# Cutting the last two result banks of a weight-gradient matmul differently: 384 + 128 columns, and two stores of 256

## The chip, the cores and the metric

One core of a Trainium2 chip. The metric is device microseconds of one execution.

The runs scatter by some 0.8 us, and the change was expected to be worth a few hundredths. So most of the argument uses an interval inside one trace, the **closing stretch**: from the start of VectorE's addition for the next to last bank to the end of the span. All that the change touches lies in it. A store **lands** when the trace shows its last completion signal.

## The reference

```python
batch, m, k, n = 16, 512, 1024, 768          # input [16, 512, 1024], grad_output [16, 512, 768], float32
grad_weight = np.einsum('bmk,bmn->kn', input, grad_output)   # [1024, 768], float32
```

That is a sum over 8192 rows, or 64 slices of 128 rows, for a result of 1024 x 768.

## The kernel before

Inputs are rounded to bf16 while they are loaded. TensorE runs 512 of the 768 columns ("wide") as eight banks of 128 x 512, one for each block of 128 result rows, and the other 256 columns ("narrow") transposed. Partial sums are added from the accumulation banks to `acc` in on-chip memory as the slices arrive. The last 14 slices (50 to 63) of the wide part are done bank by bank, so that finished banks can be stored while the others run. This loop is the whole end of the program:

```python
    def add_out(dst, src):
        nc.vector.tensor_add(out=dst, in0=src, in1=dst)
    # ... (cut: loads, rounding, the main accumulation, the narrow part and its 4 stores from ScalarE)
    for k in range(KS):                                   # KS = 8, NA = 512, NB = 256
        slices = range(parts["A" if k < KS // 2 else "B"].done, S)
        pieces = [(0, NA)] if k < KS - 1 else [(0, 256), (256, 384), (384, NA)]
        for c0, c1 in pieces:
            name = free.pop(0)
            bank = psum.tile([P, NA], f32, name=name)[:, 0 : c1 - c0]
            for s in slices:
                wide_mm(bank, k, s, s == slices[0], s == slices[-1], c0, c1)
            add_out(acc[:, k, c0:c1], bank)
            free.append(name)
            W = NB if k < 6 else c1 - c0
            for c in range(c0, c1, W):
                nc.sync.dma_start(out=OUT[:, k, c : c + W], in_=acc[:, k, c : c + W])
```

So banks 0 to 5 are stored in two halves, bank 6 in one store of 512, bank 7 in three pieces: 12 + 1 + 3 = 16 stores on SyncE's queue.

Of the kernel before, what the change touches and what calls it, by code (L numbers as in the profile page):

```python
# [9 lines left out]
NA = 512  # L10
# [16 lines left out]
def kernel(  # L27
# [13 lines left out]
    KS = K // P  # L41
    NB = N - NA
# [74 lines left out]
    def add_out(dst, src):  # L117
        nc.vector.tensor_add(out=dst, in0=src, in1=dst)  # L118
# [7 lines left out]
    def wide_mm(bank, k, s, start, stop, c0=0, c1=NA):  # L126
        nc.tensor.matmul(  # L127
            bank, xs[s][:, k * P : (k + 1) * P], gwide[s][:, c0:c1], start=start, stop=stop
        )
# [105 lines left out]

    for k in range(KS):
        slices = range(parts["A" if k < KS // 2 else "B"].done, S)
        pieces = [(0, NA)] if k < KS - 1 else [(0, 256), (256, 384), (384, NA)]
        for c0, c1 in pieces:
            name = free.pop(0)  # L240
            bank = psum.tile([P, NA], f32, name=name)[:, 0 : c1 - c0]
            for s in slices:
                wide_mm(bank, k, s, s == slices[0], s == slices[-1], c0, c1)
            add_out(acc[:, k, c0:c1], bank)
            free.append(name)
            W = NB if k < 6 else c1 - c0
            for c in range(c0, c1, W):
                nc.sync.dma_start(out=OUT[:, k, c : c + W], in_=acc[:, k, c : c + W])

# [29 lines left out]
```

## Time and profile before

| | kernel before |
|---|---|
| median of the first three runs | 176.0 us (175.91 to 176.1) |
| span in the profile | 174.27 us |
| TensorE busy | 97% of the span |
| next to last bank's addition starts | 168.41 |
| last bank's three additions start | 169.94, 170.72, 171.50 |
| last store issued, landed | 171.82, 173.36 |

The table is read as a relay. TensorE ends an accumulation, VectorE adds it within 0.02 us, SyncE issues the store 0.03 us after the addition ends, and the store lands 1.5 us or more later. Only the last runner of each kind is on the path to the end. The lines themselves are in the prediction.

### The profile page before, as it was taken

Reading aid. Unit: us, or ns where it says so; the run is one execution under the profiler, and the core shown is the slowest. Engines: PE = TensorE matmul, PEld = TensorE weight load, DVE = VectorE, ACT = ScalarE, POOL = GpSimd, SP = SyncE. Lnnn points to the kernel's source line nnn. Section 1 sums busy time; section 2 is a strip of 40 time slices with the busy share of each in tenths; the row PEclk is TensorE's granted clock in tenths of the full one; section 3 lists DMA queues with packets and bytes.
Section 4 is the critical chain, followed back from the end, with each engine's and each line's share of the span. In section 5 each row is a group of like instructions: output and inputs, shape, how many; then the busy total and the mean of one; then the engine's idle time right before and its main releaser. Section 6 shows DMA issues by size and latency. Waiting matters only on the chain.

```text
span 174.3 us, 2013 instructions
## 1 busy us (share of the span) xinstructions
PE 169.9 (97%) x793; PEld 78.4 (45%) x808; DVE 61.3 (35%) x103; ACT 6.2 (4%) x12; POOL 66.7 (38%) x129
## 2 busy tenths in 40 slices
PE   8999999999999999999999999999999999999993
PEld 3444444444444444444444444444444444444463
DVE  0655582883940039300000662200560003931122
ACT  2640000000000000000000000000000000000000
POOL 7444434444444444444444444444274200000000
PEclk9999999999999999999999999999999999999999
DMA  5999999999999999999999999999999990085623
GB/s 192 276 208 209 207 209 208 208 208 209 207 208 209 207 208 210 207 209 209 206 209 208 208 210 207 207 209 208 207 209 209 207 202 11 0 190 160 170 86 120
DMA packets 25048, 33.35 MB, mean 191 GB/s; under 512 B 6480, under 2 KB 16592, under 8 KB 25040
## 3 DMA queue, kind: packets, MB, share of 16 engines
q0 software_dynamic: 18000, 28.65, 89.9%
q10 hardware_dynamic: 4448, 2.10, 4.7%
q1 hardware_dynamic: 2592, 2.49, 4.2%
q8 instruction: 6, 0.10, 0.2%
q14 instruction: 2, 0.02, 0.0%
HBM read 58.72 MB, written 3.15 MB: 355 GB/s over the span
## 4 chain that ended last, share of the span: by engine, by line
PE 97%; issue 0%; DVE 0%
PE bank L127 63%; PE bank L134 32%; PE bank L81 3%; DVE acc L118 0%
## 5 line engine op out<-in xcount | busy, mean ns | idle before, releaser
L127 PE MATMUL bank<-gt,xt 128*128 128x512 bf16 (+2 forms) x515 | 108.3, 367 | 0.5
L127 PEld LDWEIGHTS <-xt 128*128 128x128 bf16 x524 | 50.2, 98 | 57.2
L118 DVE TENSOR_TENSOR acc<-bank,acc 128x512 f32<-128x512 f32 (+2 forms) x62 | 37.9, 667 | 73.4 <-PE bank L127 72.9
L134 PE MATMUL bank<-xt,gt 128*128 128x512 bf16 x242 | 54.8, 379 | 0.3
L97 POOL DMA_DIRECT2D xt<-in_input_dram x62 | 33.1, 533 | 38.7 <-DMA xt<-in_input_dram 36.5
L92 POOL DMA_DIRECT2D gt<-in_grad_output_dram x63 | 33.8, 536 | 31.2 <-DMA gt<-in_grad_output_dram 24.9
L134 PEld LDWEIGHTS <-gt 128*128 128x128 bf16 x252 | 24.6, 98 | 29.7
L118 DVE TENSOR_TENSOR acct<-bank,acct 128x512 f32<-128x512 f32 x24 | 15.7, 682 | 30.0 <-PE bank L134 29.9
L81 PE MATMUL bank<-const-bfloat16-1.0 128*128 128x512 bf16 (+1 forms) x12 | 4.6, 574 | 0.8 <-PEq L263 0.8
L81 PEld LDWEIGHTS <-const-bfloat16-1.0 128*128 128x128 bf16 x12 | 1.6, 140 | 3.5 <-issue 3.5
L122 DVE COPY acc<-bank 128x512 f32<-128x512 f32 x4 | 2.7, 687 | 1.0 <-PE bank L127 1.0
L180 DVE STREAM_TRANSPOSE turned<-acct 128x512 f32<-128x512 f32 x4 | 2.9, 715 | 0.1
L127 PEld LDWEIGHTS <-x 128*128 128x128 bf16 x16 | 1.6, 98 | 1.9 <-DVE x L107 0.2
L107 DVE CAST g<-gf 128x256 bf16<-128x256 f32 x2 | 0.6, 290 | 4.7 <-DMA gf<-in_grad_output_dram 4.7
L124 ACT COPY acc<-bank 128x512 f32<-128x512 f32 x4 | 2.1, 589 | 1.3 <-PE bank L127 1.3
L127 PE MATMUL bank<-gt,x 128*128 128x512 bf16 x8 | 2.1, 379 | 0.0
L127 PE MATMUL bank<-g,x 128*128 128x512 bf16 x8 | 2.0, 398 | 0.0
L122 DVE COPY acct<-bank 128x512 f32<-128x512 f32 x2 | 1.3, 686 | 1.3 <-PE bank L134 1.3
L107 ACT CAST x<-xf 128x256 bf16<-128x256 f32 x4 | 1.4, 409 | 0.0
L107 ACT ACT_TABLE_LOAD x1 | 1.3, 1283 | 1.7 <-PEq L263 1.7
L124 ACT COPY acct<-bank 128x512 f32<-128x512 f32 x2 | 1.1, 588 | 1.5 <-PE bank L134 1.5
L107 DVE CAST x<-xf 128x256 bf16<-128x256 f32 (+1 forms) x5 | 1.0, 260 | 0.0
(8 smaller groups left out, 3.3 us busy)
## 6 DMA issues: line engine op xcount, KB each, us to landing
xt<-in_input_dram POOLq DMA_DIRECT2D x62, 256.0 KB, 8.5
gt<-in_grad_output_dram POOLq DMA_DIRECT2D x63, 192.0 KB, 8.5
out_dram<-acc SPq DMA_DIRECT2D x13, 128.0 KB, 2.7
xf<-in_input_dram ACTq DMA_DIRECT2D x2, 512.0 KB, 5.1
out_dram<-turned ACTq DMA_DIRECT2D x4, 256.0 KB, 3.4
gf<-in_grad_output_dram SPq DMA_DIRECT2D x1, 256.0 KB, 3.9
out_dram<-acc SPq DMA_DIRECT2D x1, 256.0 KB, 2.0
gf<-in_grad_output_dram SPq DMA_DIRECT2D x1, 128.0 KB, 4.7
```

The costliest lines, as they stand in the source:

```text
L81: nc.tensor.matmul(wps[:, 0:cols], ones, nc.const_aps.tensor(1.0, (P, cols), bf16), start=True, stop=True,)
L92: nc.gpsimd.dma_start(out=gt, in_=G[s * P : (s + 1) * P, :])
L97: nc.gpsimd.dma_start(out=xs[s], in_=X[s * P : (s + 1) * P, :])
L107: copy(out=dst[:, c0:c1], in_=src[:, c0:c1])
L118: nc.vector.tensor_add(out=dst, in0=src, in1=dst)
L122: nc.vector.tensor_copy(out=dst, in_=src)
L124: nc.scalar.copy(out=dst, in_=src)
L127: nc.tensor.matmul(bank, xs[s][:, k * P : (k + 1) * P], gwide[s][:, c0:c1], start=start, stop=stop)
L134: nc.tensor.matmul(bank, gnarrow[s].rearrange("p (r t) -> p t r", t=NT)[:, t], xs[s][:, h * NA : (h + 1) * NA], start=start, stop=stop,)
L180: nc.vector.transpose(out=turned[:, h * hb : (h + 1) * hb, :, t], in_=dst.rearrange("p (b r) -> p b r", r=SQ),)
```

## The change

The last bank is cut in two pieces in place of three (fewer instructions and stores, the same last piece of 128), and the next to last bank goes out in two stores of 256, like those before it.

```diff
-        pieces = [(0, NA)] if k < KS - 1 else [(0, 256), (256, 384), (384, NA)]
+        pieces = [(0, NA)] if k < KS - 1 else [(0, 384), (384, NA)]
...
-            W = NB if k < 6 else c1 - c0
+            W = NB if k < KS - 1 else c1 - c0
```

## The prediction

> **What bounds the kernel now.** I read the page first (busy shares, the chain that ended last), then the end of the run: the chain in order of time, VectorE's timeline for the last 6 us, the SyncE queue, and the table of stores. The page settles the main body:
>
> ```profile
> PE 169.9 (97%) x793; PEld 78.4 (45%) x808; DVE 61.3 (35%) x103; ACT 6.2 (4%) x12; POOL 66.7 (38%) x129
> ...
> PE 97%; issue 0%; DVE 0%
> PE bank L127 63%; PE bank L134 32%; PE bank L81 3%; DVE acc L118 0%
> ```
>
> TensorE is busy 97% of the 174.3 us span and is the whole chain but for one VectorE addition. Only two things can therefore move the time: TensorE's stream, and what follows its last matmul. The chain in order of time shows where the stream stops:
>
> ```profile
> 164.76 6.72 PE bank L127 x58
> 171.48 0.02 issue
> 171.50 0.29 DVE acc L118
> ```
>
> The last matmul ends at 171.48, the last addition takes 0.29 us, and the span runs to 174.3. So there is a **tail** of 2.8 us: addition, last store, closing of the program. The change touches only what lies after about 168.4 us. VectorE's additions mark there when each accumulation is complete, because each starts within 0.02 us of its last matmul:
>
> ```profile
> 165.39 0.69 DVE L118 TENSOR_TENSOR acc<-bank,acc 128x512 f32<-128x512 f32 x1 [2.33 <-PE bank L127]
> 168.41 0.69 DVE L118 TENSOR_TENSOR acc<-bank,acc 128x512 f32<-128x512 f32 x1 [2.33 <-PE bank L127]
> 169.94 0.42 DVE L118 TENSOR_TENSOR acc<-bank,acc 128x256 f32<-128x256 f32 x1 [0.84 <-PE bank L127]
> 170.72 0.29 DVE L118 TENSOR_TENSOR acc<-bank,acc 128x128 f32<-128x128 f32 x1 [0.36 <-PE bank L127]
> 171.50 0.29 DVE L118 TENSOR_TENSOR acc<-bank,acc 128x128 f32<-128x128 f32 x1 [0.49 <-PE bank L127]
> ```
>
> Every addition waited for TensorE (the brackets), so VectorE is never behind. Differences of these starts, divided by the 14 slices of an accumulation (the trace counts 14 matmuls of 256 columns and 28 of 128), give the real cost of one matmul, which the modelled durations (379, 272 and 219 ns) do not:
> - 512 columns: (168.41 - 165.39) / 14 = 215.7 ns
> - 256 columns: (169.94 - 168.41) / 14 = 109.3 ns
> - 128 columns: (170.72 - 169.94) / 14 = 55.7 ns, and the same for the third piece.
>
> The line through the first and the last is 0.4167 ns per column plus 2.4 ns per matmul; at 256 it gives 109.1 ns. So the time goes by columns, and a piece more costs almost nothing.
>
> The last store is issued at 171.82, just after the last addition ends:
>
> ```profile
> 171.82 0.33 SPq L248 DMA_DIRECT2D out_dram<-acc  x1
> ```
>
> and the table of stores says how long each size takes from issue to landing:
>
> ```profile
> out_dram<-acc SPq DMA_DIRECT2D x1, 256.0 KB, 2.0
> ...
> out_dram<-acc SPq DMA_DIRECT2D x2, 64.0 KB, 1.5
> ```
>
> So the last 64 KB lands at about 173.3. From there to 174.3 is 1.0 us of closing, and from the span to the measured time another 1.7 us (the profiled run took 176.04). The change touches neither.
>
> **What the Trainium skill says, and whether the trace agrees.**
> - "TensorE: Matmul & The Clock Gate", section "Back-to-back issue gap", gives N / 2.4 + 2.5 ns for a warm matmul of N columns. The trace agrees: 215.7, 109.3 and 55.7 ns against 215.8, 109.2 and 55.8. The same section says that a stream of weight load and matmul pairs sustains about 81 ns at 128 columns; here the stream does 55.7, although each weight load shows 98 ns of busy time, so the loads hide even at the smallest size.
> - "Perfetto Trace Analysis", section "DMA Optimizations", says that splitting a transfer may let parts start sooner where DMA engines are idle. The DMA share in the page's slices is 9 for most of the run, but between stores at the end the engines rest (no byte moves from 168.9 to 169.6 us), so nothing there needs a split to find room.
> - "DMA: Bandwidth & Descriptors", section "Queues, rings and completion order", says that each DMA engine takes descriptors in ring order. The last store can therefore stand behind the one before it. In the trace of before no two of the last stores overlap, so it does not show this.
>
> **The change part by part.** All numbers below are on the clock of the old trace.
>
> *1. Next to last bank: two stores of 256 columns for one of 512.* Adds one issue of 0.33 us on SyncE: 169.13 to 169.46, then 169.46 to 169.79. SyncE next has work at 171.27 (below), so the issue is hidden. The bytes are the same; the old store moved its 256 KB between about 169.9 and 170.75, well before the next data. Worth 0 either way.
>
> *2. Last bank, matmuls.* Removed: 14 of 256 columns, 14 of 128. Added: 14 of 384. The last 14 of 128 stay. A 384 column matmul should take 384 x 0.4167 + 2.4 = 162.4 ns. So 14 x 162.4 = 2.27 us replaces 14 x (109.3 + 55.7) = 2.31 us: 14 matmuls' fixed 2.4 ns, **0.035 us less**, all on the path. That is the whole gain.
>
> *3. Additions.* Removed: 0.42 and 0.29 us. Added: one of 384 columns, estimated by a line through 292 ns at 128, 425 at 256 and 692 at 512 as 0.56 us. It starts at 168.41 + 2.27 = 170.68 and ends at 171.24. The last addition is due at 170.68 + 0.78 = 171.46, so VectorE is free 0.2 us before. Hidden, and the last addition is the same 128 columns and 0.29 us: done at 171.75.
>
> *4. Stores of the last bank.* Before: 128, 64, 64 KB. After: 192 and 64 KB. The 192 KB store is issued at 171.27 and holds SyncE to 171.60; the last is ready at 171.78. No wait at the issue. At the transfer it is closer: in the DMA view of these windows the first byte moves about 0.80 us after the issue, and the last about 1.3 us after it for 128 KB and 1.6 us for 256 KB. By interpolation the 192 KB store moves between 172.07 and about 172.72; the last store's bytes are due from 172.58. DMA engines that are late with the first would delay their share of the second: an estimated **0 to 0.15 us more**, by this overlap.
>
> *5. Tail.* The same last piece, so the same 1.5 us to landing and 1.0 us of closing.
>
> The sum is -0.035 + (0 to 0.15), taken as -0.035 + 0.05 = about +0.02 us on 176.0. That is no change.
>
> **The rivals.**
> - *The 192 KB store holds the last one up.* For it: the overlap just worked out, and that 0.51 us, against 0.78 before, now separates the last two issues. Against it: only the engines that are late with the larger store can pass the delay on. It would make 176.1 us, at the very most 176.2.
> - *Fewer instructions save real time*, 14 matmuls, 14 weight loads and one addition. For it: each weight load is busy for 98 ns; if the 14 removed loads were exposed at that, 1.4 us would go, and the result would be 174.6. Against it: 128 column matmuls already start every 55.7 ns, so the loads cannot be exposed.
> - *VectorE or SyncE becomes the bound at the end* through the wider addition or the later store. For it: VectorE's margin before the last addition shrinks from 0.49 to about 0.2 us, SyncE's to the same. Against it: both are still positive. If both failed by 0.1 us: 176.1.
> - *A store waits for an earlier one's semaphore.* In the compiled order of the changed kernel, the new second store of the next to last bank waits for a store issued about 9 us before; the slowest SyncE store of the old trace took 4.7 us to land, so the wait is over. If it were not, only that store would move, and it has over 2 us to spare.
>
> **Range and chances.** Centre 176.0. The known terms span -0.04 to +0.15; the runs of before span 175.91 to 176.1, and another set of runs can sit a little off. I give 175.7 to 176.3. Two per cent is 3.5 us; the whole region that the change touches, from 168.4 to the end of the stores, is 5 us, so neither side is reachable by an effect that the trace shows: faster 0.01, same 0.98, slower 0.01.
>
> **What would show each step right or wrong in the changed profile.** Step 2: the addition of 384 columns starts 2.27 us after the addition of the bank before it (3.05 us to the last addition; 3.09 before). Step 3: that addition takes 0.56 us and the last one still shows idle time before it that TensorE ended. Steps 1 and 4: SyncE shows four issues from 169.1 on, as before, two of them back to back, and the last within 0.05 us of the last addition's end; landing of the last 64 KB still about 1.5 us; 1.6 or more would mean that it queued behind the 192 KB. The prediction would be wrong if a 384 column matmul did not follow the line, or if a transfer of 1536 bytes a row went much slower than its neighbours of 1024 and 2048.

## More of the kernel before

Every run quoted is of the undisturbed (fast) state, or a single run whose granted TensorE clock was at least 0.998 of full. Single runs serve for their profile, not for their time.

## The result, and the profile after

| | before | after |
|---|---|---|
| median | 175.99 us (175.78 to 176.47, 6 runs) | 176.12 us (175.83 to 176.55, 6 runs) |
| ratio | | 1.0006, 95% interval 0.9987 to 1.0024 |
| span of the profiled run | 174.27 us | 174.78 us |
| closing stretch | 5.864 us | 5.860 us |

The ratio is the mean time of the changed kernel's fast runs over that of the other's fast runs of the same rounds, so not quite the ratio of the medians. The time is the same.

The page of the changed kernel keeps its shape, with 14 matmuls fewer:

```profile
PE 170.4 (97%) x779; PEld 77.8 (45%) x794; DVE 61.2 (35%) x102; ACT 6.2 (4%) x12; POOL 66.4 (38%) x129
```

VectorE's last additions after the change (start, duration, operation; the bracket is the idle time before it and what ended it):

```profile
165.90 0.69 DVE L118 TENSOR_TENSOR acc<-bank,acc 128x512 f32<-128x512 f32 x1 [2.33 <-PE bank L127]
168.92 0.69 DVE L118 TENSOR_TENSOR acc<-bank,acc 128x512 f32<-128x512 f32 x1 [2.33 <-PE bank L127]
171.19 0.56 DVE L118 TENSOR_TENSOR acc<-bank,acc 128x384 f32<-128x384 f32 x1 [1.58 <-PE bank L127]
171.97 0.29 DVE L118 TENSOR_TENSOR acc<-bank,acc 128x128 f32<-128x128 f32 x1 [0.22 <-PE bank L127]
```

The three steps between starts say it all: 3.02 for the bank before (as before), 2.27 for 14 matmuls of 384 columns, 0.78 for 14 of 128. The last addition still waited 0.22 us for TensorE, so VectorE did not become the bound. The last store and the table of stores (operation, size, us from issue to landing):

```profile
172.29 0.33 SPq L248 DMA_DIRECT2D out_dram<-acc  x1
```

```profile
out_dram<-acc SPq DMA_DIRECT2D x1, 192.0 KB, 1.9
...
out_dram<-acc SPq DMA_DIRECT2D x1, 64.0 KB, 1.6
```

The last 64 KB took 1.6 us where it took 1.5 before (1.567 and 1.536 in the trace's landing records). The DMA view of the last 2.9 us of stores shows what differs; each digit is the busy share of the DMA engines in a fortieth of the window, in tenths. Before, from 170.8 us:

```profile
DMA  0000007999851016983000000279730000000000
```

After, from 171.3 us:

```profile
DMA  6200000000000000006999999889830000000000
```

Before, three stores (128, 64, 64 KB) move with rests between them. After, the 192 KB and the 64 KB run into each other (the first two digits are the end of the stores before). In the DMA records the first bytes of the 64 KB move at 173.14 and the last of the 192 KB at 173.30. That is the overlap of the prediction, at its small end: 0.03 us. It repeats: in the runs below, a 64 KB last store behind one of 192 KB lands in 1.556 to 1.591 us (3 runs), and one with a rest before it in 1.521 to 1.536 (6 runs).

**Where the profiled runs differ.** All stamps of the changed trace are 0.51 us later than the old ones, and that is no effect of the change. The chain in order of time has the same first matmuls on real data in both (start, duration, what), first the kernel before:

```profile
5.42 1.95 PE bank L127 x8
```

and then the changed kernel:

```profile
5.42 2.45 PE bank L127 x8
```

These eight matmuls come 160 us ahead of the first changed instruction. The trace's clock record has full speed from 5.63 us on in one run and from 6.73 on in the other; 1.1 us more at half speed (an estimate of the speed before, from the 0.5 that the record shows after the last matmul) would cost 0.55 us. Over the 14 traces the next to last bank's addition starts anywhere from 168.17 to 168.92, with TensorE's instructions ahead of it the same in all. The moment of the clock grant is of the right size for this, but it does not explain all of it: in the run with four banks in 4 stores each (below) full speed is on record from 3.40 us on, and that addition still starts at 168.48. For the timed runs it is not shown at all, as these have no traces.

### The profile page after: what moved, and what is told of

The parts are those of the page before. It is cut to its first block, busy times and chain, and to the rows that moved or that the text cites. A ratio compares the mean times of both kernels' runs of the same rounds, so it can differ in the third digit from the quotient of the medians.

```text
span 174.8 us, 1983 instructions
## 1 busy us (share of the span) xinstructions
PE 170.4 (97%) x779; PEld 77.8 (45%) x794; DVE 61.2 (35%) x102; ACT 6.2 (4%) x12; POOL 66.4 (38%) x129
## 4 chain that ended last, share of the span: by engine, by line
PE 97%; issue 0%; DVE 0%
PE bank L127 63%; PE bank L134 31%; PE bank L81 3%; DVE acc L118 0%
## 5 line engine op out<-in xcount | busy, mean ns | idle before, releaser
L127 PEld LDWEIGHTS <-xt 128*128 128x128 bf16 x510 | 49.4, 98 | 58.0
L127 PE MATMUL bank<-g,x 128*128 128x512 bf16 x8 | 2.6, 485 | 0.0
```

What stands on the lines that cost most here:

```text
L127: nc.tensor.matmul(bank, xs[s][:, k * P : (k + 1) * P], gwide[s][:, c0:c1], start=start, stop=stop)
```

## The experiments

First theory: time goes by columns and by the size of the last piece; everything else of the last two banks is hidden. Each trace was cut at the same points. "Matmuls" is from the next to last bank's addition to the last addition, "to issue" from the end of the last addition to the issue of the last store, "landing" from there to the last landing, "closing" from that to the end of the span; the row sums to the stretch, but for rounding. The three decimals are from the stamps of the packed traces; the views show two or fewer.

| run | SyncE stores | matmuls | last addition | to issue | landing | closing | stretch |
|---|---|---|---|---|---|---|---|
| before | 16 | 3.091 | 0.292 | 0.03 | 1.536 | 0.917 | 5.864 |
| after | 16 | 3.057 | 0.291 | 0.03 | 1.567 | 0.918 | 5.860 |
| only the last bank's cut | 15 | 3.056 | 0.290 | 0.03 | 1.556 | 0.978 | 5.907 |
| only the two stores | 17 | 3.091 | 0.291 | 0.03 | 1.523 | 1.346 | 6.279 |
| last bank in one piece | 15 | 3.022 | 0.692 | 0.03 | 2.002 | 0.978 | 6.721 |
| 256 + 256 | 16 | 3.057 | 0.424 | 0.03 | 1.707 | 0.917 | 6.132 |
| 448 + 64 | 16 | 3.189 | 0.214 | 0.33 | 1.717 | 0.917 | 6.364 |
| 192 KB store from ScalarE | 15 (+1) | 3.056 | 0.292 | 0.03 | 1.591 | 0.978 | 5.944 |
| four pieces of 128 | 18 | 3.126 | 0.290 | 0.03 | 1.521 | 1.285 | 6.249 |
| 256, 128, 64, 64 | 18 | 3.127 | 0.225 | 0.18 | 1.489 | 1.284 | 6.301 |
| before, first bank in 4 stores | 18 | 3.092 | 0.292 | 0.03 | 1.528 | 1.285 | 6.224 |
| before, four banks in 4 stores | 24 | 3.092 | 0.292 | 0.03 | 1.528 | 0.917 | 5.856 |
| only the two stores, bank 5 in one | 16 | 3.091 | 0.292 | 0.03 | 1.536 | 0.916 | 5.863 |
| 256, 160, 96 | 16 | 3.091 | 0.256 | 0.03 | 1.500 | 0.916 | 5.791 |

All outputs are right.

### Each edit alone

The last bank's cut alone, against the changed kernel:

```diff
-            W = NB if k < KS - 1 else c1 - c0
+            W = NB if k < 6 else c1 - c0
```

> Only the last bank's edit (384 and 128 columns); the next to last bank keeps its one store of 512. Measured is the closing stretch, from the start of the next to last bank's addition to the end of the span: 5.86 us in the kernel before and 5.86 in the changed one. Theory (only columns and the last piece count; the stores of the next to last bank are hidden): last addition 3.05 us after the next to last bank's, landing 1.6, stretch 5.86, the same as with both edits. Rival (the second store of the next to last bank is what gave back the 0.04 us): stretch 5.82.

Measured 5.907: neither number. Matmuls and landing are as the theory said; what is new is 0.06 us in the closing, which I had taken for a constant.

The two stores alone:

```diff
-        pieces = [(0, NA)] if k < KS - 1 else [(0, 384), (384, NA)]
+        pieces = [(0, NA)] if k < KS - 1 else [(0, 256), (256, 384), (384, NA)]
```

> Only the next to last bank's edit (two stores of 256); the last bank keeps its pieces of 256, 128 and 128. Theory: last addition 3.09 us after the next to last bank's, landing 1.5, stretch 5.86, as the kernel before. Rival (the extra store costs 0.04): stretch 5.90.

Measured 6.279. Both theories miss, by 0.4 us, and again the whole surplus is in the closing: matmuls, addition and landing are those of the kernel before. So each edit alone makes the end longer, and together they do not. The first theory had no place for that.

### The size of the last piece

One piece, and two halves, against the changed kernel:

```diff
-        pieces = [(0, NA)] if k < KS - 1 else [(0, 384), (384, NA)]
+        pieces = [(0, NA)] if k < KS - 1 else [(0, NA)]
```

> The last bank in one piece of 512 with one store. Theory: matmuls 14 x 215.7 ns = 3.02 us (0.07 less than before), addition 0.69 in place of 0.29, landing 2.0 in place of 1.5: stretch 5.86 - 0.07 + 0.40 + 0.5 = 6.69, and some 0.8 us more than the kernel before in the timed runs (ratio about 1.005). Rival (each piece has a hidden fixed cost of tenths of a us, so cutting is nearly free of effect): stretch 6.2 or less, ratio under 1.002.

Measured stretch 6.721, median 176.92 against 176.06 us, ratio 1.004 (1.0027 to 1.0054). The lines show the two terms, the wider last addition and the longer landing:

```profile
168.58 0.69 DVE L118 TENSOR_TENSOR acc<-bank,acc 128x512 f32<-128x512 f32 x1 [2.33 <-PE bank L127]
171.60 0.69 DVE L118 TENSOR_TENSOR acc<-bank,acc 128x512 f32<-128x512 f32 x1 [2.33 <-PE bank L127]
```

```profile
out_dram<-acc SPq DMA_DIRECT2D x1, 256.0 KB, 2.0
```

```diff
-        pieces = [(0, NA)] if k < KS - 1 else [(0, 384), (384, NA)]
+        pieces = [(0, NA)] if k < KS - 1 else [(0, 256), (256, NA)]
```

> The last bank in two pieces of 256. Theory: last piece doubles, matmuls 0.035 less than before, addition 0.42 in place of 0.29, landing 1.7 in place of 1.5: stretch 5.86 - 0.035 + 0.13 + 0.2 = 6.16. Rival (number of pieces counts, size of the last does not): as the changed kernel, which also has two pieces, 5.86.

Measured 6.132, 0.03 off the theory. Two pieces and 16 stores, as the changed kernel has, but 0.27 us longer: the size of the last piece counts, not the number of pieces. The rivals of both runs fall.

### Where the hiding ends

```diff
-        pieces = [(0, NA)] if k < KS - 1 else [(0, 384), (384, NA)]
+        pieces = [(0, NA)] if k < KS - 1 else [(0, 448), (448, NA)]
```

> The last bank in pieces of 448 and 64. The margins of the changed kernel run out here on purpose. Theory (VectorE, then SyncE, then the transfer become the wait once the last piece is shorter than the work of the one before): matmuls 2.65 + 0.41 us; addition of 448 takes 0.63, so the last addition starts 3.27 after the next to last bank's and not 3.06; SyncE still issues the first store, so the last goes out about 0.33 after the first; its bytes stand behind 224 KB: landing 1.8 or more, stretch 6.2 to 6.3. Rival (a smaller last piece always ends earlier): addition 0.22 in place of 0.29 and a shorter landing, stretch 5.75.

Measured 6.364, a little over the theory; the rival is out. The lines by shape (operation, count, busy us, mean ns, idle time before) have the idle time of the last addition at 0.0, so VectorE was late for it, and then SyncE was late for the store (0.33 us "to issue" in the table):

```profile
L118 DVE TENSOR_TENSOR acc<-bank,acc 128x448 f32<-128x448 f32 x1 | 0.6, 625 | 2.0 <-PE bank L127 2.0
...
L118 DVE TENSOR_TENSOR acc<-bank,acc 128x64 f32<-128x64 f32 x1 | 0.2, 214 | 0.0
```

Three terms were off and partly cancel: the last addition began 0.08 us before the end that the profile gives for the one ahead of it; SyncE needed 0.43 us from one issue to the next, not 0.33, with a semaphore check between the two in the trace; and the landing was 1.717, not 1.8 or more. The landing still shows what a larger store just ahead costs: the same 32 KB landed in 1.489 us with a rest before it (the run with 256, 128, 64 and 64, below).

### The overlap of the last two stores

```diff
-                nc.sync.dma_start(out=OUT[:, k, c : c + W], in_=acc[:, k, c : c + W])
+                queue = nc.scalar if (k, c0) == (KS - 1, 0) else nc.sync
+                queue.dma_start(out=OUT[:, k, c : c + W], in_=acc[:, k, c : c + W])
```

> The changed kernel with the 192 KB store of the last bank issued from ScalarE's queue, the last 64 KB store alone on SyncE. Theory (the last store's landing grew from 1.5 to 1.6 because its bytes stood behind the 192 KB on the same engines): the two queues share the engines, so the last 64 KB can slip in between and land in about 1.5, or the 192 KB ends last instead; stretch 5.80 to 5.90. Rival (the 0.04 us come from SyncE's issue of 0.33 us just before): SyncE is free, stretch 5.82 with landing 1.5.

Measured 5.944, above both. The last 64 KB landed in 1.591 us, not faster than in one queue (1.567), so neither SyncE's issue nor the order within one queue is what adds to the 1.52 to 1.54 of a 64 KB store that has the engines to itself. What remains, by elimination, is that both transfers move at the same time; how the DMA engines interleave them was not tested. The other 0.06 us are again in the closing.

### More pieces

```diff
-        pieces = [(0, NA)] if k < KS - 1 else [(0, 384), (384, NA)]
+        pieces = [(0, NA)] if k < KS - 1 else [(0, 128), (128, 256), (256, 384), (384, NA)]
```

> The last bank in four pieces of 128. Theory: one piece more than the kernel before costs 14 x 2.4 ns = 0.035: last addition 3.12 us after the next to last bank's, landing 1.5, stretch 5.89. Rival (a hidden fixed cost of a piece, store or semaphore of 0.1 us or more): stretch 5.96 or more.

Measured 6.249. The matmul term is right to 0.01 us (3.126), so a piece costs only its 14 short fixed parts. The number is the rival's: something that comes with a store or a semaphore costs 0.37 us.

```diff
-        pieces = [(0, NA)] if k < KS - 1 else [(0, 384), (384, NA)]
+        pieces = [(0, NA)] if k < KS - 1 else [(0, 256), (256, 384), (384, 448), (448, NA)]
```

> A try for the best end: pieces of 256, 128, 64 and 64. Theory: a 64 column matmul follows the line, 64 x 0.4167 + 2.4 = 29 ns, so matmuls 3.12; last addition 0.22, landing 1.45: stretch 5.86 + 0.035 - 0.07 - 0.05 = 5.78, ratio 0.9995, not to be told from 1 in the timed runs. Rival (weight loads of 98 ns busy can no longer hide behind 29 ns, say 50 ns each pair): last addition 0.6 us later, stretch 6.4.

Measured 6.301, ratio 1.0015 (1.0002 to 1.0028): the try at a better end is slower, by 0.15%, far under the two per cent at which a run is called slower. The rival's reason is wrong, as 14 matmuls of 64 columns took 0.41 us, 29 ns each, on the line. The excess is 0.37 us of closing and 0.15 us in which SyncE was not ready (0.18 from the end of the last addition to its store).

### The closing: a second theory

The closing came out at 0.917 with 16 stores, 0.978 with 15, 1.346 with 17, 1.285 with 18. The first theory, in which it is a constant, is wrong. A semaphore is a counter with which a transfer reports that it is done. In the trace, SyncE ends by checking the semaphores of all stores in one fixed order, some 0.06 us apart. Stores and the early loads that SyncE and ScalarE issue take eight semaphores in turn (so the compiled instruction order has it). With 16 stores on SyncE the last store is on the semaphore that is checked last: by the time it lands, all others have been checked. With 17 the last store is on the first of the eight: SyncE stands at that check until it lands, and has seven more to make. The stamps of the packed trace name the semaphores, which the views leave out. In all 14 runs the last eight checks are of semaphores 107, 109, 110, 111, 114, 115, 116 and 117, in this order. The last store reports on 117 with 16 or 24 SyncE stores, on 116 with 15, on 107 with 17 and on 109 with 18.

The views show the number of SyncE's closing semaphore checks that are left after the last landing; each window ends just after the last of the eight (L274 is the end of the program; operation, count, duration in ns, first and last start). The kernel before:

```profile
L274 SPq EVENT_SEMAPHORE  x1: 28/28/28, 173.4 to 173.4; - x1
```

The changed kernel:

```profile
L274 SPq EVENT_SEMAPHORE  x1: 28/28/28, 173.9 to 173.9; - x1
```

The run with only the two stores:

```profile
L274 SPq EVENT_SEMAPHORE  x8: 27/28/28, 173.6 to 174.0; - x8
```

One check against eight. (1.346 - 0.917) / 7 is 0.061 us for a check; 15 stores leave one more (0.978), 18 leave six (0.917 + 0.37 = 1.28).

SyncE's count alone decides only because the other transfers that take a turn (2 loads on SyncE, 2 loads and 4 stores on ScalarE) are eight in every run but one. The exception is the run with the 192 KB store from ScalarE: 24 transfers in all, as in the kernel before, but ScalarE's store has 117 there and the last SyncE store 116, so it closes like 15 stores (0.978). What decides is the place of the last store's own semaphore in the order of the checks.

That theory was fitted to these runs, so it was then tested on others. The next four are edits of the kernel **before**.

```diff
-            W = NB if k < 6 else c1 - c0
+            W = P if k < 1 else NB if k < 6 else c1 - c0
```

> The kernel before with its first bank (stored some 17 us before the end of the additions) written in four stores of 128 columns, so 18 SyncE stores and not 16; nothing in the last two banks differs. New theory: SyncE's closing sequence checks the stores' semaphores in a fixed order, 0.061 us each; stores take eight semaphores in turn, so with 18 stores the last one uses a semaphore with six checks still to come. Closing (last landing to end) 0.917 + 6 x 0.061 = 1.28, stretch 6.23, some 0.37 us more in the timed runs. Rival (an extra store near the end is what cost 0.4 us in the earlier runs): closing 0.92, stretch 5.86.

Measured closing 1.285, stretch 6.224; median 176.61 against 176.08 us, ratio 1.0024 (1.0007 to 1.0041). Nothing near the end was touched:

```profile
L274 SPq EVENT_SEMAPHORE  x7: 28/28/28, 173.5 to 173.9; - x7
```

Seven checks, the store's own and six more. Two extra stores some 17 us earlier cost what two extra pieces at the end did (1.285 in both).

```diff
-            W = NB if k < 6 else c1 - c0
+            W = P if k < 4 else NB if k < 6 else c1 - c0
```

> The kernel before with its first four banks in four stores each: 24 SyncE stores, again a multiple of eight. Theory: the last store is on the semaphore checked last, closing 0.917, stretch 5.86, in spite of eight more stores. Rival (each store more than 16 adds its own check at the close): 0.917 + 8 x 0.061 = 1.40, stretch 6.35.

Measured closing 0.917, stretch 5.856. Eight more stores cost nothing, because 24 is again a multiple of eight:

```profile
L274 SPq EVENT_SEMAPHORE  x1: 28/28/28, 173.4 to 173.4; - x1
```

```diff
-            W = NB if k < 6 else c1 - c0
+            W = NB if k < 5 or k == 6 else c1 - c0
```

> The run with two stores of 256 for the next to last bank and pieces of 256, 128 and 128 for the last, which came out at a stretch of 6.28 with 17 stores, made 16 again by one store of 512 for the bank before those. Theory: closing back to 0.917, stretch 5.86. Rival (two stores of the next to last bank beside three of the last cost 0.4 by themselves): stretch 6.28.

Measured closing 0.916, stretch 5.863. The two stores of the next to last bank are free once the count is 16, so the cost of that edit alone was the count.

### A better end by the trace

```diff
-        pieces = [(0, NA)] if k < KS - 1 else [(0, 256), (256, 384), (384, NA)]
+        pieces = [(0, NA)] if k < KS - 1 else [(0, 256), (256, 416), (416, NA)]
```

> A try for a better end with 16 stores: pieces of 256, 160 and 96. Theory: matmuls as before, last addition 96 columns, 0.26 in place of 0.29, landing about 1.51, closing 0.917: stretch 5.81. In the timed runs no difference that can be told from 1. Rival (SyncE's minimum of about 0.47 us between two stores, or the 96 column matmuls off the line, hold it): stretch 5.86 or more.

Measured stretch 5.791, 0.07 us less than either kernel; the addition and the landing gave 0.036 each:

```profile
171.07 0.33 DVE L118 TENSOR_TENSOR acc<-bank,acc 128x160 f32<-128x160 f32 x1 [0.54 <-PE bank L127]
171.66 0.26 DVE L118 TENSOR_TENSOR acc<-bank,acc 128x96 f32<-128x96 f32 x1 [0.27 <-PE bank L127]
```

The timed runs do not see it: median 176.08 against 176.08 us, ratio 0.9997 (0.9981 to 1.0014). It is better in the one interval that was traced, and not shown to be faster.

## Why the prediction was right or wrong

The median lay in the range (176.12 in 175.7 to 176.3; of the single runs one, at 176.55, did not), and the two per cent class is the forecast one. With an effect this small the timed runs can't tell a right mechanism from a wrong one, so each step is judged by the traces. The readings and sums of the prediction hold when they are redone, but two are rounded freely: the closing is 0.92 us and not 1.0, and from the span to the time of the profiled run it is 1.77 us and not 1.7. Point by point:

- **Step 1, two stores for one: right only beside the other edit.** The issue and the transfer were hidden, as said. But "worth 0 either way" holds only while the count of stores is kept: by itself the edit made the closing stretch 0.42 us longer.
- **Step 2, matmuls: right.** -0.035 us predicted, 3.091 to 3.057 measured. The straight line in columns also held at 64 columns (29 ns), outside the range that it came from.
- **Step 3, additions: right.** 0.56 us for 384 columns, hidden, with a margin of 0.22.
- **Step 4, the last two stores: right mechanism, upper half of the range not needed.** 0.03 us of the "0 to 0.15"; the sum had taken 0.05. The 192 KB moved from 0.83 to 1.52 us after its issue, where 0.80 to 1.45 was interpolated.
- **Step 5, the tail: right for this change by luck.** "1.0 us of closing" stands there as a thing that the change does not touch. It was 0.917 in both kernels because one store was added and one removed. The prediction looked at semaphores as what a store may wait for at its issue, and not as what the program checks at its end. A prediction of either edit alone, made by the same steps, would have been wrong by 0.06 or 0.4 us, still within two per cent.
- **Rivals.** The 192 KB store holding the last one up is real and of 0.03 us. Instructions saved bring their 2.4 ns each and no more. VectorE and SyncE as the bound need a last piece of 64: shown with 448 + 64. The check of an earlier store's semaphore is in the trace, but it held up nothing that counts: the second store of the next to last bank went out 0.38 us after the first, and its issue took 0.43 us where 0.33 was expected, over 1 us before SyncE's next store.
- **The sum.** +0.02 us predicted, -0.004 measured in the stretch. The 0.13 us between the medians are within the scatter, whose interval reaches from -0.13% to +0.24%.

## What to carry to other kernels

When a kernel is bound by one engine to its last 3 us, cutting the last result differently can move only what lies there. In these runs that was mostly the addition and the landing of the last piece, up to the cut (448 + 64) where VectorE and SyncE are late for it. Measure these inside one trace, as the runs scatter by more. Check the semaphores at the end as well: where stores take them in turn and the program checks them in a fixed order, the place of the last store's semaphore decides how many checks follow the last landing, and every store or load that takes a turn shifts it. Two edits that look independent can share such a count, so try each alone.

## What the Trainium skill lacked or had wrong

- No page tells how a program's closing checks depend on the semaphore of the last store. Measured: 0.061 us a check, closing 0.917 us with 16 or 24 stores, 0.978 with 15, 1.346 with 17, 1.285 with 18.
- "TensorE: Matmul & The Clock Gate", section "Back-to-back issue gap": its figures for a stream of weight load and matmul pairs, about 81 ns at 128 columns and about 131 ns at 512, are both off here: 55.7 and 215.7 ns. It gives N / 2.4 + 2.5 for isolated matmuls only and says that this over-counts at large N; in this stream of pairs the formula fits all of 64 (29 ns), 128, 256, 384 and 512.
- "DMA: Bandwidth & Descriptors", section "Latency and other measured facts": about 0.6 us to the first byte on these queues, without saying from where it is counted. Here the first packet of a last store moved 0.83 us after the start of its issue instruction, or 0.50 us after the end of it.
- The same page, section "Anatomy of one DMA — SWDGE (gpsimd) path", fits time to size for transfers issued from GpSimd; no page has such a fit for SyncE's. For stores issued from SyncE onto idle engines the runs show 1.50 us for 48 KB, 1.52 to 1.54 for 64 KB, 1.71 for 128 KB and 2.00 for 256 KB.
